# Sums of the up and down weights formed in DRAM by copies and adding transfers, in a fast-multiplication decoder layer on one core

## The chip, the cores and the metric

The kernel runs on one core of one Trainium2 chip. The metric is device time in microseconds (us); the kernel before took 1193.68 us, the median of three runs (1193.61 to 1193.87).

## The reference

One decoder layer over a sequence of 1024 positions and a model width of 1024, in float32. What matters here is its second half; the first half (attention over a window of 128, a spatial gating unit, two sigmoid gates, output projection) is computed as before.

```
merged = sigmoid(g_a) * (y_att @ w_oa) + sigmoid(g_b) * (y_sgu @ w_ob)
x = x + merged @ w_out
h = rmsnorm(x)
z = h @ w_up                              # 1024 x 5632
zc = causal depthwise convolution of z over 3 positions, plus a bias
gate, val = split(zc)                     # 2816 each
x = x + (silu(gate) * val) @ w_down       # 2816 x 1024
```

## The kernel before, in words

Every float32 operand is split into a high and a low part, and a product is three matmuls: high x high, high x low, low x high. The gate projections, the up projection and the down projection multiply two-by-two block matrices with seven block products instead of eight (a Strassen scheme of Winograd's form). So sums of weight blocks (S1 to S4) and sums of activation blocks (T1 to T4) stand beside the blocks themselves (A11 to A22, B11 to B22), and the products are put together by additions (`u2`, `x7`, `g0`, `g1`, `v0`, `v1`).

From v_phase on all engines run in the order in which the program is written; nothing is reordered. TensorE does the matmuls, VectorE (DVE) the sums of products, the convolution and some splits, ScalarE (ACT) the high parts and activations, GpSimd (POOL) the low parts and some weight sums. All transfers are issued by SyncE (SP) on one queue, and SP waits in order for whatever a transfer needs. The stages, one after the other:

- **Attention and SGU**, to about 221 us.
- **Gates** (`v_end`, `gate_pair`): eight pairs of gate tiles of 84 matmuls each. Per pair `load_p` and `load_q` bring the weights (`lp`, `lq`). POOL makes S3 and S1 from them (`sums_q`), then the low parts `pl` and `s3l`, then S2 and S4 (`sums_r`), then `ql` and the low part of S2 and S4 (`gax`). The gates' results go out to DRAM as `dth`.
- **Branches** (`branch`, `run_jobs`): sixteen tiles of 24 matmuls. For tile n SP loads a gate tile two ahead (`th`, 512 KB, 3 buffers) and a weight block four ahead (`wj`, 256 KB, tag `raw`, 3 buffers). ACT and POOL split the block two ahead (`wjh`, `wjl` at line 108, 2 buffers). DVE multiplies and adds.
- **Out** (`out_tile`, `last_tile`): eight tiles of 48 matmuls with weights of 512 KB; their results are normalized and split, with the sums T1 to T4.
- **Up** (`first_pair`, `fast_pair`): 22 pairs of column blocks of 84 matmuls each, in the order `U_ORDER`. `Left` holds one pair's weights: `p` (A11, A12), `q` (S1 and A22), `s3`, and `r` (S2, S4; made by POOL at line 620 through `sub`). Here S1 and S3 are read from DRAM (`load_q`, `load_s3`). `keep_act` writes the activations and their sums to DRAM.
- **Down** (`mlp`): seven block products M1 to M7, each over eleven blocks of 128 rows taken two at a time (a "group"). `loads` brings a group's weights and activations, `prep` splits them.

**Where the sums come from.** For the up stage, `sums_load` loads 256 KB and 512 KB of a pair's weights into a tile `ls` (2 buffers), `sums_step` makes two sums on DVE (line 620) and stores them as `sum<i>` in DRAM, 512 KB. `sums_step` runs twice in each of the gate pairs 2 to 7 and in ten of the sixteen branches. For the down stage `sum_loads` loads A21 and A22 of a group while M1 and M2 run, `sums2` makes S2 from them, and `prep` makes S3, S4 and S1, all on DVE. A11 and S2 stay in SBUF.

Of the kernel before, what the change touches and what calls it, by code (L numbers as in the profile page):

```python
# [10 lines left out]
F = mybir.dt.float32  # L11
# [30 lines left out]
def body(ctx, tc, nc, a):  # L42
# [217 lines left out]
    st = {}  # L260

# [360 lines left out]

    def x_gain(r, ks):
        for k in ks:
            x = xr_raw[r][:, k, :]
            nc.scalar.activation(x, x, AF.Copy, scale=cp[:, 186 + 4 * r + k:187 + 4 * r + k])

    def x_sums(ks, first):
        for k in ks:
            x0 = xr_raw[0][:, k, :]  # L630
            if first:
                sub(nc.vector, x0[:, L], x0[:, H], x0[:, L])
            else:
                x1 = xr_raw[1][:, k, :]
                sub(nc.vector, x0[:, H], x1[:, H], x0[:, H])
                sub(nc.vector, x1[:, H], x1[:, H], x0[:, L])
                sub(nc.vector, x1[:, L], x1[:, L], x1[:, H])
# [181 lines left out]
    def v_end():  # L819
# [53 lines left out]
        sums_load()  # L873
# [11 lines left out]
        nc.vector.tensor_tensor(x7, x7, e, op=ALU.add)  # L885
        nc.vector.tensor_tensor(q.g1, x5, q.g1, op=ALU.add)
        nc.vector.tensor_tensor(q.v1, x7, q.v1, op=ALU.add)
        nc.vector.tensor_tensor(q.v0, q.u2, q.v0, op=ALU.add)
# [39 lines left out]
    class Left:  # L928
# [8 lines left out]
        def load_q(self):  # L937
            if self.i is None:
                self.q = wload(self.sq, "lq")
                return  # L940
            self.q = raw("lq")
            nc.sync.dma_start(self.q[:, 0:4], pools["sum"][self.i][:, 1])
            nc.sync.dma_start(self.q[:, 4:8], self.sq[:, 4:8])

        def load_s3(self):
            self.s3 = pools["wx"].tile([128, 4, 128], F, tag="s3", name=nm("s3"))
            nc.sync.dma_start(self.s3, pools["sum"][self.i][:, 0])
# [9 lines left out]
        def sum_s3(self):  # L957
            self.s3 = s3_pool.tile([128, 4, 128], F, tag="s3", name=nm("s3"))
            sub(nc.gpsimd, self.s3, self.p[:, 0:4], self.q[:, 0:4])

        def sum_f3(self):

            sub(nc.gpsimd, self.p[:, 0:4], self.q[:, 4:8], self.r[:, 0:4])
# [15 lines left out]
        def sum_s2(self):  # L979
            self.r = raw("lr")  # L980
            sub(nc.gpsimd, self.r[:, 0:4], self.q[:, 0:4], self.p[:, 0:4])

        def sum_s4(self):
            sub(nc.gpsimd, self.r[:, 4:8], self.p[:, 4:8], self.r[:, 0:4])
# [26 lines left out]
    class Blocks:  # L1011
# [23 lines left out]
        def sums(self, x1, x7, m4):  # L1035

            nc.vector.tensor_tensor(self.v1, x1, self.v1, op=ALU.add)
            nc.scalar.copy(self.u2, self.v1)
            nc.vector.tensor_tensor(self.v0, self.u2, m4, op=ALU.add)
            nc.vector.tensor_tensor(self.v1, x7, self.v1, op=ALU.add)  # L1040
            self.scale(self.zv)
# [7 lines left out]

    sums = {"load": 0, "make": 0}  # L1050

    def sums_load():

        i = sums["load"]
        if i < NPAIR:
            x = pools["ls"].tile([128, 3, 4, 128], F, tag="ls", name=nm("ls"), bufs=2)
            nc.sync.dma_start(x[:, 0], a["wup"][2 * i][:, 0:4])
            nc.sync.dma_start(x[:, 1:3], a["wup"][2 * i + 1].rearrange("p (b k) m -> p b k m", b=2))
            sums[i] = x
            sums["load"] += 1  # L1060

    def sums_step():

        i = sums["make"]
        if i < NPAIR:
            sums_load()
            x = sums.pop(i)
            sub(nc.vector, x[:, 0], x[:, 0], x[:, 1])
            sub(nc.vector, x[:, 1], x[:, 1], x[:, 2], ALU.add)
            t = pools["dr"].tile([128, 2, 4, 128], F, tag=f"sum{i}", name=f"sum{i}")  # L1070
            nc.sync.dma_start(t, x[:, 0:2])
            pools.setdefault("sum", {})[i] = t
            sums["make"] += 1

# [27 lines left out]
    def gate_pair(c, prev):  # L1102
# [16 lines left out]
        if c > 1:  # L1119
            sums_step()  # L1120
# [75 lines left out]
    def branch(n):  # L1196
        br, c = B_ORDER[n]

        def main(w):
# [14 lines left out]
            if n % 2 == 0 or n in (5, 9):  # L1214
                sums_step()
# [38 lines left out]
    HK = NPAIR // 2  # L1254
# [11 lines left out]
    def out_tile(i):  # L1266
        d = D_ORDER[i]

        def main(w):
# [20 lines left out]
            if d < 4:  # L1290
                eng = nc.gpsimd if i < 6 else nc.vector
                right_split("B11", k, h[:, L], eng)
                sub(nc.vector, h[:, L], h[:, H], h[:, L])
                right_split("T1", k, h[:, L], eng)
            else:
                g = hs_[k]
                sub(nc.vector, g[:, H], h[:, H], g[:, H])
# [3 lines left out]
                t2 = sub(nc.vector, pools["raw2"][:, k, :], h[:, H], g[:, L])  # L1301
                sub(nc.vector, pools["raw4"][:, k, :], h[:, L], t2)
# [7 lines left out]
    def last_tile(w, ac):  # L1310
# [28 lines left out]
        sub(nc.vector, g[:, H], h[:, H], g[:, H])  # L1339
        right_split("B22", k, h[:, H], nc.vector)  # L1340
        right_split("T3", k, g[:, H], nc.vector)
        t2 = sub(nc.vector, pools["raw2"][:, k, :], h[:, H], g[:, L])
        sub(nc.vector, pools["raw4"][:, k, :], h[:, L], t2)
# [63 lines left out]
    def keep_act(i, tv):  # L1407
# [9 lines left out]
        if row == 0:  # L1417
            put("B11", tv[:, L])
            t1 = sub(nc.vector, tt(), tv[:, H], tv[:, L])
            put("T1", t1)  # L1420
            pools["prev"] = (tv, t1)
        else:
            g, t1 = pools["prev"]
            put("B21", tv[:, L])
            put("B22", tv[:, H])
            put("T3", sub(nc.vector, g[:, H], tv[:, H], g[:, H]))
# [4 lines left out]
    U_ORDER = [i for j in range(HK) for i in (j, j + HK)]  # L1431
    lefts = [Left(a["wup"][2 * i], a["wup"][2 * i + 1], i) for i in U_ORDER]

    def first_left():

        w = lefts[0]
        w.load_p()
        w.load_s3()
        w.load_q()
        yield  # L1440
        w.split_p()

    def first_pair():
# [32 lines left out]
        nc.vector.tensor_tensor(x7, x7, u2, op=ALU.add)  # L1476
# [11 lines left out]
        nc.vector.tensor_tensor(q.v1, u2, x7, op=ALU.add)  # L1488
        nc.vector.tensor_tensor(q.v0, u2, q.v0, op=ALU.add)
# [10 lines left out]
    def fast_pair(n, prev, q, hooks, rms=None):  # L1500
# [43 lines left out]
        nc.vector.tensor_tensor(x7, x7, q.g1, op=ALU.add)  # L1544
# [8 lines left out]
        if nx:  # L1553
            nx.split_q()
            nx.split_r(n + 1)
        else:
# [8 lines left out]
    SUM_AT = (2, 4, 5, 7, 8, 10)  # L1565
# [5 lines left out]
    def mlp():  # L1571
        groups = [(s, k0, k1) for s in STEPS for k0, k1 in GR]
        blk, ring = {}, {}
        zz = []

        def block(n, k0, k1):

            if k0 < 8:
                if n not in blk:
                    blk[n] = Y(n, F, [128, 8, 512])  # L1580
                return blk[n][:, k0:k1, :]
            if not zz:
                zz.append(pools["ex"].tile([128, 8, 512], F, tag="T3", name="zz"))
            b = 3 * ("A11", "S2").index(n) - 8
            return zz[0][:, b + k0:b + k1, :]

        def slot(n, dt, cnt):

            if n not in ring:
                y = pools["yd"].tile([128, 8, 512], F, name="rs") if n == "rs" else Y(n, dt, [128, 8, 512])  # L1590
                ring[n] = [y, 0]
# [3 lines left out]

        def a_in(n, t, k0, k1):
            r, c = int(n[1]) - 1, int(n[2]) - 1
            for k in range(k0, k1):
                nc.sync.dma_start(t[:, k - k0, :], a["wdown"][k + HK * c][:, 512 * r:512 * r + 512])

        raw_ = {}

        def loads(g):
# [15 lines left out]
        pre = {}  # L1619

        def sum_loads(k0, k1):
            pre[k0] = (block("S2", k0, k1), slot("rs", F, k1 - k0))
            a_in("A21", pre[k0][0], k0, k1)
            a_in("A22", pre[k0][1], k0, k1)

        def sums2(k0, k1):

            c, x = pre.pop(k0)
            sub(nc.vector, c, c, x, ALU.add)
            sub(nc.vector, c, c, block("A11", k0, k1))  # L1630

        def prep(g):
# [56 lines left out]
        def plus(n, d, p, last=False):  # L1689

            t = rs[n][:, d, :]
            nc.vector.scalar_tensor_tensor(t, p, 0.5, t, op0=ALU.mult, op1=ALU.add)
# [3 lines left out]
        def done(s):  # L1696
            for d in range(4):
# [4 lines left out]
                if s == "M6":  # L1702
                    plus("C21", d, X[d])
# [4 lines left out]
                if s == "M5":  # L1708
                    plus("C22", d, X[d], True)
# [33 lines left out]
        for g in range(len(groups)):  # L1743
# [5 lines left out]
            if g in SUM_AT:  # L1749
                sum_loads(*GR[SUM_AT.index(g)])  # L1750
# [16 lines left out]
            if g - 2 in SUM_AT:  # L1767
                sums2(*GR[SUM_AT.index(g - 2)])
# [12 lines left out]
def layout(x, mix_norm, w_in, q_norm, k_norm, sinks, sgu_norm, w_s, b_s,  # L1781
# [18 lines left out]
    wup = tiles(w_up, 8)[up_order]  # L1800

    def pcol(v):
# [10 lines left out]
    ali = -slopes[None, :, None] * dist[:, None, :]  # L1813
    return {
# [9 lines left out]
        "wup": wup,  # L1824
        "wdown": c(w_down.reshape(NPAIR, 128, 1024)),
# [20 lines left out]
```

## Time and profile before

| | before |
|---|---|
| time, median of 3 runs | 1193.68 us (1193.61 to 1193.87) |
| the profiled execution: its time / its span | 1193.8 us / 1192.1 us |
| TensorE (PE) busy | 1180.0 us, 99% of the span |
| VectorE (DVE) busy | 877.8 us, 74% |
| ScalarE (ACT) busy | 541.8 us, 45% |
| GpSimd (POOL) busy | 567.4 us, 48% |
| DMA, one queue | 190.26 MB, 45.9% of 16 engines' span |

The span runs from the first to the last instruction; the time also holds what lies around it. An engine's busy time is the sum of its instructions' spans. PEld is TensorE's loading of weights, which runs beside its matmuls. "DMA share" is the mean busy share of the core's 16 DMA engines. In rows of instructions the first column is the start in us, the second the duration; an arrow in brackets names what ended the idle time before.

### The profile page before, as it was taken

What the parts mean: (1) busy time and instruction counts of PE and PEld (TensorE: products, weight loads), DVE (VectorE), ACT (ScalarE), POOL (GpSimd) and SP (SyncE); (2) the same over time, 40 slices, a digit from 0 to 9 for tenths busy, and PEclk for the clock granted to TensorE, in tenths of its full rate; (3) what the DMA queues carried; (4) which work ended last, traced back from release to release, by engine and by line L of the source; (5) the groups of instructions that cost most, each with busy time, mean ns of one, the idle gap of its engine ahead of it and who ended that gap; (6) DMA issues with size and microseconds to landing.
All of it is one profiled execution on the core that took longest, in us unless ns stands there. A gap on an engine that the chain in (4) does not pass through costs nothing.

```text
span 1192.1 us, 15888 instructions
## 1 busy us (share of the span) xinstructions
PE 1180.0 (99%) x5890; PEld 1000.9 (84%) x5890; DVE 877.8 (74%) x1028; ACT 541.8 (45%) x832; POOL 567.4 (48%) x364
## 2 busy tenths in 40 slices
PE   8999999999999999999999999999999999999998
PEld 8989989988888888888888888888888888888887
DVE  7798975745638565668897788878788798865674
ACT  8555567644335222234544444444444445434331
POOL 2367685487768222343756575656657551000000
PEclk9999999999999999999999999999999999999999
DMA  7110133037786997342143342423333258966471
GB/s 272 35 54 19 54 136 130 5 130 260 245 315 212 347 327 278 125 165 100 54 142 108 104 143 98 148 91 124 108 131 124 89 209 290 373 230 194 151 233 67
DMA packets 79134, 191.27 MB, mean 160 GB/s; under 512 B 8913, under 2 KB 9169, under 8 KB 79057
## 3 DMA queue, kind: packets, MB, share of 16 engines
q1 hardware_dynamic: 79056, 190.26, 45.9%
q8 instruction: 46, 0.75, 0.3%
q14 instruction: 32, 0.25, 0.1%
HBM read 139.63 MB, written 50.59 MB: 160 GB/s over the span
## 4 chain that ended last, share of the span: by engine, by line
PE 89%; DVE 4%; POOL 1%; issue 1%; ACT 0%; POOLq 0%; DVEq 0%; ACTq 0%
PE pz L1028 48%; PE pd L1672 10%; PE pdy L1672 8%; PE px L93 2%; PE px L92 2%; PE po L93 2%; PE po L92 2%; PE po L91 2%; PE px L91 2%; PE pvs L91 1%; PE pvs L92 1%; PE pvs L93 1%; DVE ya L529 1%; PE pq L91 1%; PE pq L93 1%; PE pq L92 1%
## 5 line engine op out<-in xcount | busy, mean ns | idle before, releaser
L1028 PE MATMUL pz<-T,qh 128*128 128x512 f32 x472 | 145.6, 390 | 0.0
L988 POOL TENSOR_TENSOR pl<-lp,ph 128x1024 fp32r<-128x1024 f32 x30 | 72.5, 2418 | 83.5 <-ACT ph L87 83.3
L1028 PE MATMUL pz<-B,ph 128*128 128x512 f32 x352 | 109.1, 391 | 0.0
L1028 PEld LDWEIGHTS pz<-T,qh 128*128 128x128 f32 x472 | 88.5, 188 | 18.6 <-ACT u L879 0.3
L1028 PE MATMUL pz<-T,ql 128*128 128x512 f32 x236 | 91.8, 389 | 0.0
L108 POOL TENSOR_TENSOR wjl<-wj,wjh 128x512 fp32r<-128x512 f32 (+1 forms) x24 | 40.6, 1692 | 95.8 <-ACT wjh L87 95.8
L988 POOL TENSOR_TENSOR ql<-lq,qh 128x1024 fp32r<-128x1024 f32 x30 | 76.9, 2565 | 9.1 <-ACT qh L87 9.1
L1028 PEld LDWEIGHTS pz<-B,ph 128*128 128x128 f32 x352 | 65.3, 188 | 15.0 <-ACT x L1519 1.8
L1044 DVE TENSOR_TENSOR pz<-pz,rstd_b 128x1024 f32<-128x1024 f32 x60 | 73.9, 1232 | 4.2 <-ACT rstd_b L141 2.1
L988 POOL TENSOR_TENSOR s3l<-s,s3h 128x512 fp32r<-128x512 f32 x29 | 39.8, 1373 | 69.7 <-ACT s3h L87 69.7
L1028 PE MATMUL pz<-T,s3h 128*128 128x512 f32 x232 | 71.4, 389 | 0.0
L1028 PE MATMUL pz<-B,pl 128*128 128x512 f32 x176 | 68.6, 390 | 0.0
L1672 PE MATMUL pd<-bl,ah 128*128 128x512 f32 x176 | 68.5, 389 | 0.0
L1672 PE MATMUL pd<-bh,ah 128*128 128x512 f32 x176 | 68.5, 389 | 0.0
L1672 PE MATMUL pd<-bh,al 128*128 128x512 f32 x176 | 68.5, 389 | 0.0
L1028 PE MATMUL pz<-T,AX 128*128 128x512 f32 x264 | 63.4, 389 | 0.0
L1028 PE MATMUL pz<-B,AX 128*128 128x512 f32 x264 | 63.4, 389 | 0.0
L1028 PEld LDWEIGHTS pz<-T,AX 128*128 128x128 f32 x264 | 49.6, 188 | 10.3
L1028 PEld LDWEIGHTS pz<-B,AX 128*128 128x128 f32 x264 | 49.6, 188 | 10.3
L1378 DVE SCALAR_TENSOR_TENSOR tg<-pz,cp,tg 128x1023 f32<-128x1023 f32 (+1 forms) x44 | 56.2, 1278 | 0.8
L1378 DVE SCALAR_TENSOR_TENSOR tv<-pz,cp,tv 128x1023 f32<-128x1023 f32 (+1 forms) x44 | 56.2, 1277 | 0.8
L988 POOL TENSOR_TENSOR AX<-lr,AX 128x1024 fp32r<-128x1024 f32 x22 | 53.7, 2440 | 5.1 <-ACT AX L87 5.1
(342 smaller groups left out, 3511.8 us busy)
## 6 DMA issues: line engine op xcount, KB each, us to landing
ls<-wup SPq DMA_DIRECT2D x22, 512.0 KB, 5.3
sum<-ls SPq DMA_DIRECT2D x22, 512.0 KB, 5.3
lp<-wup SPq DMA_DIRECT2D x22, 512.0 KB, 3.6
ra<-wdown SPq DMA_DIRECT2D x44, 256.0 KB, 4.6
b<-T SPq DMA_DIRECT2D x44, 256.0 KB, 3.8
B<-tv SPq DMA_DIRECT2D x33, 256.0 KB, 2.0
T<-tt SPq DMA_DIRECT2D x33, 256.0 KB, 2.0
b<-B SPq DMA_DIRECT2D x33, 256.0 KB, 3.1
```

The lines of the kernel that those rows point to most:

```text
L91: nc.tensor.matmul(out, wh, mh, start=first, stop=False, **kw)
L92: nc.tensor.matmul(out, wh, ml, start=False, stop=False, **kw)
L93: nc.tensor.matmul(out, wl, mh, start=False, stop=last, **kw)
L108: nc.gpsimd.tensor_tensor(l[:, :nk, :], r[:, :nk, :], h[:, :nk, :].bitcast(F), op=ALU.subtract)
L529: nc.vector.tensor_tensor(ya[r, 2 * half:2 * half + 2, b * 128:(b + 1) * 128], p[r, g], o[r], op=ALU.add)
L988: nc.gpsimd.tensor_tensor(l, r, h.bitcast(F), op=ALU.subtract)
L1028: nc.tensor.matmul(o, p[:, k, :], y[:, q, k, :], start=not more and k == 0 and j == 0, stop=k == 3 and j == 2, skip_group_check=True)
L1044: nc.vector.tensor_tensor(z, z, rstd_b, op=ALU.mult)
L1378: nc.vector.scalar_tensor_tensor(t[:, j:], p[:, 0:1024 - j], cw[:, ci, 2 - j:3 - j], t[:, j:], op0=ALU.mult, op1=ALU.add)
L1672: nc.tensor.matmul(o[d], p[:, k - k0, m], q[:, k - k0, :], start=new and k == 0 and j == 0, stop=k == HK - 1 and j == 2, skip_group_check= ...
```

## The change

Three edits belong together.

1. **The sums for the up stage.** DVE no longer makes them. For pair i, ACT issues a copy of two blocks of `w_up` (512 KB) within DRAM into `sum<i>`, and POOL issues a transfer that adds two other blocks to it there. The copies run up to three pairs ahead of the adds; an add waits for its copy. `sums_step` now runs once in each of gate pairs 1 to 7 and once in each branch. The tile `ls` and its loads and stores are gone. The blocks of `w_up` lie in memory in a new order, so that one transfer covers two of them; `load_p` reads two pieces of 2 KB per partition where it read one of 4 KB.
2. **The sums for the down stage.** In the up stage `fast_pair` calls `down_step` once per pair: 12 copies on ACT (1 MB, the last ones 512 KB) and 18 adds on POOL (1 MB or 512 KB, the last ones half). All of S1 to S4 then lie in DRAM. `loads` reads each group's weights, block or sum, in one transfer into the ring `ra`; `sum_loads`, `sums2` and the subtractions in `prep` are gone.
3. **Signs.** The transfers can add but not subtract, so some sums of weights change sign. The sums of activations and the additions of products change sign with them: a `tensor_tensor` with its operands swapped or with add for subtract, and in 19 places `neg_sum`, a `scalar_tensor_tensor`, for a subtraction.

The matmuls, their number and their order are the same.

```diff
+    def rows4k(t):
+        return t.rearrange("(p b) m -> p (b m)", b=2)
+    todo = {"copy": 0, "add": 0}
+    def sums_step():
+        j = todo["add"]
+        while todo["copy"] < min(j + 3, NPAIR):
+            sum_copy(U_ORDER[todo["copy"]])
+            todo["copy"] += 1
+        if j < NPAIR:
+            sum_add(U_ORDER[j])
+            todo["add"] += 1
+    def sum_copy(i):
+        sums[i] = dr.tile([256, 512], F, tag=f"sum{i}", name=f"sum{i}")
+        nc.scalar.dma_start(rows4k(sums[i]), rows4k(a["wup"][i, 0:2].rearrange("b p m -> (b p) m")))
+    def sum_add(i):
+        nc.gpsimd.dma_start(rows4k(sums[i]), rows4k(a["wup"][i, 1:3].rearrange("b p m -> (b p) m")), accum_op=ALU.add, max_dma_last_dim=4096)
...
+    def neg_sum(out, x, y):
+        nc.vector.scalar_tensor_tensor(out, x, -1.0, y, op0=ALU.mult, op1=ALU.subtract)
+        return out
...
@@ Left
-            nc.sync.dma_start(self.q[:, 0:4], pools["sum"][self.i][:, 1])
-            nc.sync.dma_start(self.q[:, 4:8], self.sq[:, 4:8])
+            nc.sync.dma_start(self.q[:, 0:4], sums[self.i][128:256])
+            nc.sync.dma_start(self.q[:, 4:8], self.sq)
...
@@ gate_pair
         gate_out(("b", c - 1), prev.zg)
-        if c > 1:
-            sums_step()
+        sums_step()
         q.prod(q.v0, "S3", "T3")
...
-        nc.vector.tensor_tensor(x7, x7, q.g1, op=ALU.add)
+        sub(nc.vector, x7, x7, q.g1)
         if nx:
             nx.sums_r()
-        if c > 1:
-            sums_step()
...
@@ branch
-            if n % 2 == 0 or n in (5, 9):
-                sums_step()
+            sums_step()
...
@@ keep_act
-            t2 = sub(nc.vector, tt(), tv[:, H], t1)
+            t2 = neg_sum(tt(), t1, tv[:, H])
             put("T2", t2)
-            put("T4", sub(nc.vector, tt(), tv[:, L], t2))
+            put("T4", sub(nc.vector, tt(), tv[:, L], t2, ALU.add))
...
+    D_ADDS = [(i, j) for j in range(6) for i in range(3)]
+    D_COPIES = [(i, j) for j in range(6) for i in (1, 0)]
+    def down_copy(i, j):
+        t = d_sum[i, j] = dr.tile([256, 1024 if j < 5 else 512], F, tag=f"sd{i}{j}", name=f"sd{i}{j}")
+        nc.scalar.dma_start(t, wd(j, i, i + 2))
+    def down_add(i, j):
+        x, y = d_sum[1, j], d_sum[0, j]
+        out, src = ((x, wd(j, 2, 4)), (y[128:256], x[128:256]), (y[0:128], y[128:256]))[i]
+        nc.gpsimd.dma_start(out, src, accum_op=ALU.add, max_dma_last_dim=4096)
+    def down_step(n):
+        if n < len(D_COPIES):
+            down_copy(*D_COPIES[n])
+        if 0 <= n - 2 < len(D_ADDS):
+            down_add(*D_ADDS[n - 2])
...
@@ fast_pair
             nx.split_q()
             nx.split_r(n + 1)
+            down_step(n - 1)
...
@@ mlp
-            x = None
-            if s == "M1":
-                x = block("A11", k0, k1)
-                a_in("A11", x, k0, k1)
-            elif s not in ("M5", "M6"):
-                x = slot("ra", F, n)
-                a_in({"M2": "A12", "M7": "A22", "M4": "A22", "M3": "A12"}[s], x, k0, k1)
+            x = slot("ra", F, n)
+            a_in(LHS[s], x, k0, k1)
...
-            if s == "M6":
-                x = block("S2", k0, k1)
-            elif s in ("M7", "M3"):
-                sub(nc.vector, x, x, block("S2", k0, k1))
-            elif s == "M5":
-                x = block("A11", k0, k1)
-                sub(nc.vector, x, x, block("S2", k0, k1), ALU.add)
...
-            if g in SUM_AT:
-                sum_loads(*GR[SUM_AT.index(g)])
...
-            if g - 2 in SUM_AT:
-                sums2(*GR[SUM_AT.index(g - 2)])
```

More of the change, by code (lines that the diff above doesn't have):

```diff
@@ L260, in body @@
     st = {}
+    sums = {}
+    HK = NPAIR // 2
+    U_ORDER = [i for j in range(HK) for i in (j, j + HK)]
+    def rows4k(t):
[14 more added lines that the diff above has]
+        nc.gpsimd.dma_start(rows4k(sums[i]), rows4k(a["wup"][i, 1:3].rearrange("b p m -> (b p) m")), accum_op=ALU.add, max_dma_last_dim=4096)
     def q_proj(n):
@@ L1038, in sums @@
             nc.scalar.copy(self.u2, self.v1)
[L1039 to L1040 removed]
+            sub(nc.vector, self.v0, m4, self.u2)
+            sub(nc.vector, self.v1, x7, self.v1)
             self.scale(self.zv)
@@ L1048, in last_sum @@
             self.scale(self.zg)
[L1050 to L1073, printed above, removed]
     jobs.clear()
@@ L1300, in main @@
                 right_split("T3", k, g[:, H], nc.vector)
-                t2 = sub(nc.vector, pools["raw2"][:, k, :], h[:, H], g[:, L])
-                sub(nc.vector, pools["raw4"][:, k, :], h[:, L], t2)
+                t2 = neg_sum(pools["raw2"][:, k, :], g[:, L], h[:, H])
+                sub(nc.vector, pools["raw4"][:, k, :], h[:, L], t2, ALU.add)
             if i == 0:
@@ L1338, in last_tile @@
         g = hs_[k]
-        sub(nc.vector, g[:, H], h[:, H], g[:, H])
+        sub(nc.vector, g[:, H], g[:, H], h[:, H])
         right_split("B22", k, h[:, H], nc.vector)
         right_split("T3", k, g[:, H], nc.vector)
-        t2 = sub(nc.vector, pools["raw2"][:, k, :], h[:, H], g[:, L])
-        sub(nc.vector, pools["raw4"][:, k, :], h[:, L], t2)
+        t2 = neg_sum(pools["raw2"][:, k, :], g[:, L], h[:, H])
+        sub(nc.vector, pools["raw4"][:, k, :], h[:, L], t2, ALU.add)
     late = {}
@@ L1425, in keep_act @@
             put("B22", tv[:, H])
-            put("T3", sub(nc.vector, g[:, H], tv[:, H], g[:, H]))
-            t2 = sub(nc.vector, tt(), tv[:, H], t1)
+            put("T3", sub(nc.vector, g[:, H], g[:, H], tv[:, H]))
+            t2 = neg_sum(tt(), t1, tv[:, H])
             put("T2", t2)
-            put("T4", sub(nc.vector, tt(), tv[:, L], t2))
-    U_ORDER = [i for j in range(HK) for i in (j, j + HK)]
-    lefts = [Left(a["wup"][2 * i], a["wup"][2 * i + 1], i) for i in U_ORDER]
+            put("T4", sub(nc.vector, tt(), tv[:, L], t2, ALU.add))
+    lefts = [Left(a["wup"][i, 0::3].rearrange("b p m -> p b m"), a["wup"][i, 2], i) for i in U_ORDER]
     def first_left():
@@ L1475, in first_pair @@
         nx.split_s3()
-        nc.vector.tensor_tensor(x7, x7, u2, op=ALU.add)
+        sub(nc.vector, x7, x7, u2)
         q.prod(q.g1, "S4", "B22", more=True)
@@ L1487, in first_pair @@
         q.u2 = u2
-        nc.vector.tensor_tensor(q.v1, u2, x7, op=ALU.add)
-        nc.vector.tensor_tensor(q.v0, u2, q.v0, op=ALU.add)
+        sub(nc.vector, q.v1, x7, u2)
+        sub(nc.vector, q.v0, q.v0, u2)
         def rms():
@@ L1543, in fast_pair @@
             nx.split_p()
-        nc.vector.tensor_tensor(x7, x7, q.g1, op=ALU.add)
+        sub(nc.vector, x7, x7, q.g1)
         if rms:
@@ L1572, in mlp @@
         groups = [(s, k0, k1) for s in STEPS for k0, k1 in GR]
[L1573 to L1585, printed above, removed]
+        ring = {}
         def slot(n, dt, cnt):
             if n not in ring:
-                y = pools["yd"].tile([128, 8, 512], F, name="rs") if n == "rs" else Y(n, dt, [128, 8, 512])
-                ring[n] = [y, 0]
+                ring[n] = [Y(n, dt, [128, 8, 512]), 0]
             y, i = ring[n]
@@ L1594, in slot @@
             return y[:, 2 * (i % 4):2 * (i % 4) + cnt, :]
+        SRC = {"A12": 0, "A11": 1, "A22": 3, "S3": (1, 0), "S1": (1, 1), "S4": (0, 0), "S2": (0, 1)}
         def a_in(n, t, k0, k1):
-            r, c = int(n[1]) - 1, int(n[2]) - 1
-            for k in range(k0, k1):
-                nc.sync.dma_start(t[:, k - k0, :], a["wdown"][k + HK * c][:, 512 * r:512 * r + 512])
+            j = k0 // 2
+            if n[0] == "A":
+                src = wd(j, SRC[n], SRC[n] + 1)
+            else:
+                i, b = SRC[n]
+                src = d_sum[i, j][128 * b:128 * b + 128]
+            nc.sync.dma_start(t.rearrange("p k m -> p (k m)"), src)
         raw_ = {}
@@ L1687, in put, with plus @@
             nc.sync.dma_start(a["out"][4 * r + d, :, 512 * c:512 * c + 512], t)
-        def plus(n, d, p, last=False):
+        def plus(n, d, p, last=False, by=0.5):
             t = rs[n][:, d, :]
-            nc.vector.scalar_tensor_tensor(t, p, 0.5, t, op0=ALU.mult, op1=ALU.add)
+            nc.vector.scalar_tensor_tensor(t, p, by, t, op0=ALU.mult, op1=ALU.add)
             if last:
@@ L1702, in done @@
                 if s == "M6":
-                    plus("C21", d, X[d])
+                    plus("C21", d, X[d], by=-0.5)
                 if s == "M7":
@@ L1708, in done @@
                 if s == "M5":
-                    plus("C22", d, X[d], True)
+                    plus("C22", d, X[d], True, -0.5)
                 if s == "M3":
```

55 lines of the change are left out of this document (25 added, 30 removed).

## The prediction

> **What bounds the kernel now.** I read the page's first part, then busy time by stage, then the chain of waits, then the DMA view of the stage that the change loads most.
>
> ```profile
> span 1192.1 us, 15888 instructions
> ...
> PE 1180.0 (99%) x5890; PEld 1000.9 (84%) x5890; DVE 877.8 (74%) x1028; ACT 541.8 (45%) x832; POOL 567.4 (48%) x364
> ```
>
> The profiled execution took 1193.8 us, 1.7 more than its span and 0.1 above the median of the three runs (1193.68); the sum below is made against 1193.8. The two stretches of the next view cut the span where the TensorE stops waiting.
>
> ```profile
> core 0: us, PE busy (x) PEld busy (x) DVE busy (x) ACT busy (x) POOL busy (x), PEclk, DMA share, GB/s
> 0.00:200.00 200.00, 192.05 (x1407) 179.69 (x1408) 156.33 (x319) 127.42 (x333) 116.29 (x124) 1.00 0.29 104
> 200.00:1186.00 986.00, 986.00 (x4478) 819.99 (x4478) 718.80 (x707) 414.41 (x499) 451.09 (x240) 1.00 0.50 172
> ```
>
> From 200 us to 1186 us TensorE is busy for 986.00 of 986 us. All of its idle time lies in the first 200 us (8.0 us, start and attention) and after the last matmul. A busy engine could still be a slowed one, so I took its pace from the chain of waits:
>
> ```profile
> 244.64 136.26 PE pz L1028 x600
> ...
> 580.39 397.86 PE pz L1028 x1752
> 978.24 29.92 PE pd L1672 x132
> ...
> 1185.91 2.73 DVE res L1692 x4
> ```
>
> Per matmul that is 136.26/600 = 0.2271 us in the gates, 397.86/1752 = 0.2271 in the up stage and 29.92/132 = 0.2267 in the down stage. If 0.2267 is the floor, 2352 matmuls hide 0.0004 x 2352 = 0.9 us. **So the change can win about 1 us**: no matmul is removed, and whatever is taken from VectorE (DVE) or from SP's queue comes out of engines that TensorE does not wait for. What it can lose is open.
>
> **The change part by part: what goes away.** The 44 halves of the up sums:
>
> ```profile
> L620 DVE TENSOR_TENSOR ls<-ls 128x512 f32<-128x512 f32 x44 | 44.5, 1010 | 9.4 <-DMA ls<-wup 8.6
> L620 DVE TENSOR_TENSOR tt<-tv,tt 128x512 f32<-128x512 f32 x22 | 35.8, 1625 | 0.4
> L1692 DVE SCALAR_TENSOR_TENSOR res<-pd,res 128x512 f32<-128x512 f32 x12 | 8.2, 691 | 13.3 <-PE pd L1672 13.3
> ```
>
> 44.5 us leave DVE in gates and branches, and 30 subtractions leave it in the down stage. TensorE ran full beside all of them: 0 us. The signs cost nothing either: an add for a subtract is the same instruction; the 19 `neg_sum` replace subtractions (mean 1.625 us, row two) by an operation whose nearest row of that size is 0.691. Even twice 1.625 would put 1.6 us into a pair of 19 us, of which DVE is idle for 3.4 (up stage, 296.55 of 360 in the rows below). The down stage reads as many bytes as before (77 blocks of 256 KB), two to a transfer.
>
> ```profile
> 247.00:380.50 133.50, 133.50 (x590) 110.54 (x589) 75.15 (x78) 58.82 (x72) 102.68 (x59) 1.00 0.68 233
> 380.50:468.00 87.50, 87.50 (x387) 72.47 (x386) 54.51 (x55) 20.06 (x26) 28.34 (x18) 1.00 0.85 309
> ...
> 600.00:960.00 360.00, 360.00 (x1587) 297.01 (x1586) 296.55 (x284) 163.33 (x190) 221.35 (x113) 1.00 0.35 117
> 978.00:1186.00 208.00, 208.00 (x919) 171.88 (x918) 143.77 (x140) 82.16 (x92) 7.55 (x4) 1.00 0.65 221
> ```
>
> These rows are gates, branches, up and down stage; the columns from the third on are busy PE, PEld, DVE, ACT, POOL, then clock, DMA share and GB/s. Full speed of the transfers is 309/0.85 = 363 GB/s, so a plain 512 KB (0.524 MB) costs **1.44 us** of all DMA engines, 256 KB 0.72.
>
> **What is added: where the transfers land.** `sums_step` runs once in each of gate pairs 1 to 7 and once in each branch: gates get 9 copies and 7 adds, branches 13 copies (in branches 0 to 12) and 15 adds; the up stage gets 12 copies (11.5 MB) and 18 adds (11.5 MB). No row shows a copy from DRAM to DRAM or an add. A copy is bounded by 1.44 (one pass) and 2.88 (its read and its write each paid); an add, which reads two sources and writes one, by 1.44 and 4.32. A copy is nearest to a load, 1.44. An add is nearest to two loads, 2.88. Both ends stay for the range.
>
> Gates: the old sums there were 15.2 MB of 31.1, so 15.9 MB (44 us) stay; even 9 x 2.88 + 7 x 4.32 = 56 us more make 100 of 133.5. Up stage, over 381 us: 117 GB/s is 44.6 MB; counting copies twice and adds three times (57 MB) gives 102 of 138. Both fit, hidden beside TensorE. **The branches are the tight place:**
>
> ```profile
> DMA packets 8994, 27.00 MB, mean 309 GB/s; under 512 B 1008, under 2 KB 1008, under 8 KB 8988
> ...
> th<-dth SPq DMA_DIRECT2D x16, 512.0 KB, 6.2
> sum<-ls SPq DMA_DIRECT2D x10, 512.0 KB, 5.2
> ls<-wup SPq DMA_DIRECT2D x9, 512.0 KB, 5.3
> ls<-wup SPq DMA_DIRECT2D x9, 256.0 KB, 4.4
> wj<-woa SPq DMA_DIRECT2D x7, 256.0 KB, 6.3
> ```
>
> The old sums are 10 x 0.524 + 9 x 0.786 = 12.3 of these 27 MB. In their place come 28 transfers of 0.524, 14.7 MB if each counted once. Per branch of 5.44 us the DMA engines get `th` and `wj`, 1.44 + 0.72 = 2.16, plus 1.44 + 2.88: **6.48 us of work**, 1.04 too much, in 13 branches 13.5 us.
>
> What this costs TensorE is less, since loads run ahead:
>
> ```profile
> 429.72 0.63 ACT L87 ACTIVATE wjh<-wj 128x512 fp32r<-128x512 f32 x1 [1.05 <-PE po L92]
> 435.16 0.63 ACT L87 ACTIVATE wjh<-wj 128x512 fp32r<-128x512 f32 x1 [4.81 <-PE po L92]
> ...
> 430.43 1.30 POOL L108 TENSOR_TENSOR wjl<-wj,wjh 128x512 fp32r<-128x512 f32 x1 [4.10 <-ACT wjh L87]
> ```
>
> A branch starts near 429.7, the next 5.44 later; the split of the block for the branch after is ready at 431.73, 3.4 us before that branch. The block four ahead is loaded from the moment its slot is free (2.0 into a branch) and wanted three branches later, 14.3 us on; landing takes 6.3, which leaves 8.0, and with the 3.4 it may be 11.4 us late, once. Queued behind one copy and one add (4.32) it has 7.1 left. 13.5 - 7.1 = **6.4 us** of TensorE waiting.
>
> By the Trainium skill (DMA: Bandwidth & Descriptors, Issuing engines are not separate DMA queues) transfers started by ACT, SP or GpSimd run on the same 16 engines and interleave, so moving the sums off SP's queue buys no bandwidth. No trace here shows another queue than SP's. If the rule failed, and the added queues had engines of their own, the 6.4 us would be 0.
>
> **What is added: waits and issue.** In pair 1 three copies are issued at once on ACT and the first add waits on POOL for the first of them. Behind it on POOL stand the sums and splits for pair 2:
>
> ```profile
> 254.18 1.02 ACT L1083 ACTIVATE th<-pz 128x1024 f32<-128x1024 f32 x1
> ...
> 254.79 2.42 POOL L988 TENSOR_TENSOR gax<-lr,gax 128x1024 fp32r<-128x1024 f32 x1
> 259.10 1.29 POOL L620 TENSOR_TENSOR s<-lp,lq 128x512 f32<-128x512 f32 x1 [1.88 <-DMA lq<-wga]
> 260.46 1.29 POOL L620 TENSOR_TENSOR lq<-lq 128x512 f32<-128x512 f32 x1
> 261.71 2.40 POOL L988 TENSOR_TENSOR pl<-lp,ph 128x1024 fp32r<-128x1024 f32 x1
> ...
> 266.68 0.19 PEld L1028 LDWEIGHTS pz<-x,pl 128*128 128x128 f32 x1
> ```
>
> The copy is issued at 255.2. How long 512 KB take to land, and an issue on a free and on a crowded queue, stand in the view of DMA issues and in SP's timeline:
>
> ```profile
> x<-ac SPq DMA_DIRECT2D x8, 512.0 KB, 2.7
> ```
>
> ```profile
> 270.37 0.33 SPq L97 DMA_DIRECT2D lq<-wga  x1
> ...
> 272.75 2.04 SPq L1058 DMA_DIRECT2D ls<-wup  x1
> ```
>
> Between 2.7 and the 6.2 of `th` above it lands at 257.9 to 261.4, middle 259.7. What an add holds POOL for is not shown: below it costs an issue of SP (0.33), above twice the longer POOL split here (4.8); I take the short split, 1.3. POOL resumes at 261.0 rather than 259.1, 1.9 late, and `pl` was done 2.6 before PEld took it (266.68 - 264.11): 0. At the upper ends POOL is 7.1 late, 4.5 us lost. I charge **0.6**, since `lq` itself now shares the engines with three copies. Later adds find their copy 38 us old in the gates, about 11 in the branches. In a branch POOL has 1.3 of 5.44 us to do, so an add up to 4.1 us is hidden; in the up stage 221.35 of 360 leaves 7.3 us of each pair of 19.05, in the gates 102.68 of 133.5 leaves 4.4. ACT's copies are 0.33 to 2.04 us of issue beside 20.06 of 87.5 us busy: hidden.
>
> The Trainium skill (DMA: Bandwidth & Descriptors, Specifications) gives about 1 us to the first byte of a transfer issued from GpSimd; that as price would also be hidden.
>
> **Sum:** 1193.8 + 0 (DVE, signs, down stage) + 0.6 (first add) + 6.4 (branches) = **1200.8 us**.
>
> **Rivals.**
> 1. *It fits, no slower.* If the two transfers of a branch cost under 4.0 us together, 13 x (2.16 + 4.0 - 5.44) = 9.4 less the remaining cushion of 7.4 is 2 us or less. For it: at 1.44 each the branch needs 5.04 of 5.44, and 0.85 share already ran without a stall. Against: an add has two sources. It gives 1194.4.
> 2. *Every pass through DRAM is paid.* Copy 2.88, add 4.32: 13 x (9.36 - 5.44) = 51 less 4.2, so 1241; half way up (copy 2.16, add 3.6), 13 x 2.48 = 32 less 5.6, 1221. For it: both ends of these transfers are DRAM, of none in the trace. The Trainium skill (DMA: Bandwidth & Descriptors, Latency and other measured facts) has 214 GB/s for copies from HBM to HBM, 2.45 us for 512 KB as an estimate; with an add of 2.88 that would be 1215.
> 3. *POOL is held.* An add that keeps POOL over 4.1 us (slow issue, or waiting on landings) delays `wjl` in 15 branches: at 6 us 15 x (1.3 + 6 - 5.44) = 28 less 3.4 gives 1219. Against: POOL is idle for two thirds of the stage.
> 4. *Faster.* Only through the first 200 us, which the change barely touches, or the 0.9 us of pace.
>
> **How the numbers follow.** Forecast, 1196.2 to 1208: 0.38. Rival 1: 0.34. Rival 2, from 1208 up: 0.18. Rival 3: 0.06. Rival 4: 0.04. A measurement here tells 0.2% (2.4 us) from no change. Slower 0.38 + 0.18 + 0.06 = 0.62, same 0.34, faster 0.04. The range 1193.0 to 1218.0 leaves out rival 4 and about half of rivals 2 and 3, 0.16.
>
> **What would show it.** Right: TensorE gaps between 380 and 500 us that end on ACT `wjh` or POOL `wjl`, behind them a late `wj`; DMA share near 1 there; gates, up and down stage still without a gap. Rival 1: no gap, share below 1. Rival 2: gaps of 2 us and more in each branch. Rival 3: a gap released by POOL while `wj` had landed long before. Wrong altogether: gaps in the up stage, or a different pace per matmul.

## The result, and where the profile after puts the time

The changed kernel takes **1231.6 us**, the median of four runs (1230.4 to 1232.9), against 1193.6 for the kernel before on the same chip: 1.0319 times as long (95% interval 1.0301 to 1.0337), and above the range that was forecast. The profiled execution took 1232.9 us, 39.1 more than that of before. First the head of the page of the changed kernel:

```profile
span 1231.2 us, 15752 instructions
...
PE 1194.5 (97%) x5890; PEld 1005.5 (82%) x5890; DVE 804.4 (65%) x954; ACT 542.0 (44%) x832; POOL 591.8 (48%) x404
```

DVE lost 73 us of work, and the matmuls are as many as before; still TensorE is busy 14.5 us longer, with 24.6 us more of idle span. So part of the loss is idle time and part is a slower pace. Busy time by stage shows where (branches, out, up and down stage; columns as before):

```profile
385.00:480.00 95.00, 92.96 (x404) 75.03 (x403) 40.51 (x32) 19.31 (x25) 36.03 (x32) 1.00 1.03 320
480.00:583.00 103.00, 103.00 (x470) 85.73 (x469) 77.06 (x68) 38.29 (x51) 45.29 (x24) 1.00 0.33 116
583.00:1016.00 433.00, 410.54 (x1755) 333.03 (x1754) 329.00 (x314) 181.12 (x211) 255.13 (x141) 0.98 0.56 165
1020.00:1225.00 205.00, 204.41 (x902) 168.69 (x901) 107.78 (x107) 79.33 (x90) 5.08 (x2) 1.00 0.64 221
```

The same stretch of the up stage in the kernel before:

```profile
580.40:978.20 397.80, 397.80 (x1753) 328.11 (x1753) 329.58 (x315) 181.99 (x212) 241.31 (x123) 1.00 0.36 121
```

**Nearly all of it lies in the up stage.** Its matmuls took 397.8 us and now take 433.0, 35.2 more: 433.0 - 410.5 = 22.5 us of gaps, and 410.5 - 397.8 = 12.7 us of slower matmuls at a granted clock of 0.98. The branches lost 2.0 us in gaps and 404 x 0.2271 = 91.7 of 93.0 in pace, 3.3 in all; the down stage 0.6. That is the 39.1. The DMA share of the up stage is only 0.56, so the stage didn't run out of DMA engines. The waits of the up stage say who was late:

```profile
ACT s3h L87 <- DMA s<-sum: 70.7, 15, 8.9
PE pz L1056 <- ACT x L1554: 21.9, 8, 5.6
```

(waiter, releaser: us in all, times, longest.) TensorE waited eight times for ScalarE's copy `x7` (line 1554), and ScalarE had waited for the load `s` (S3 of the next pair), one of the sums that the change forms by transfers. In the kernel before that wait was 4.8 us in all. The timeline of one pair, cut to the instructions that matter, shows the order of events:

```profile
637.56 0.50 ACTq L1449 DMA_DIRECT2D sd<-wdown  x1
639.91 0.32 SPq L970 DMA_DIRECT2D lq<-sum  x1
640.27 2.98 SPq L971 DMA_DIRECT2D lq<-wup  x1
642.18 0.95 POOL L1455 DMA_DIRECT2D sd<-wdown  x1
643.30 0.43 SPq L975 DMA_DIRECT2D s<-sum  x1
652.58 0.63 ACT L87 ACTIVATE s3h<-s 128x512 fp32r<-128x512 f32 x1 [7.66 <-DMA s<-sum]
653.11 0.57 ACT L1554 COPY x<-pz 128x512 f32<-128x512 f32 x1
...
653.73 0.77 PE L1056 MATMUL pz<-T,qh 128*128 128x512 f32 x2 [4.28 <-ACT x L1554]
```

`down_step` issues a 1 MB copy on ACT and a 1 MB add on POOL at the end of a pair, within 6 us of SP's loads `lq` and `s` for the next pair. `s` reaches ACT at 652.5. ACT's queue is in order, so the copy that TensorE needs stands behind the split of `s`. How the pace fell: the 5 us behind this gap, and the 5 us behind the next one, of 1.36 us:

```profile
653.73:658.73 5.00, 5.00 (x15) 3.97 (x16) 4.05 (x5) 2.39 (x3) 3.91 (x3) 0.66 0.15 57
676.03:681.03 5.00, 5.00 (x22) 4.14 (x23) 3.94 (x4) 2.92 (x3) 3.90 (x3) 1.00 0.14 54
```

Behind the gap of 4.28 us TensorE is busy for the whole 5 us and does 15 matmuls instead of 22, at a granted clock of 0.66: 1.6 us more lost. Behind the other long gaps (5.59, 5.04 and 3.27 us) it does 13, 12 and 15, at 0.56, 0.50 and 0.66; behind the four short ones (0.49 to 1.36 us) it does 22 at 1.00. The four long gaps so cost 33 matmuls, 7.5 of the 12.7 us, some 1.9 us each on top of their idle time. The rest is spread over the stage and was not traced. The Trainium skill (TensorE: Matmul & The Clock Gate, HAM oscillation) warns of TensorE idle for over about 3.4 us, after which the clock starts low. Three of the four long gaps agree; the one of 3.27 us lowered the clock as well, so here that length is no sharp limit (experiment 5 has a gap of 1.79 us that did).

### The profile page after: what moved, and what is told of

Its sections match the earlier page's. It is cut to its first block, busy times and chain, and to the rows that moved or that the text cites. A ratio compares the mean times of both kernels' runs of the same rounds, so it can differ in the third digit from the quotient of the medians.

```text
span 1231.2 us, 15752 instructions
## 1 busy us (share of the span) xinstructions
PE 1194.5 (97%) x5890; PEld 1005.5 (82%) x5890; DVE 804.4 (65%) x954; ACT 542.0 (44%) x832; POOL 591.8 (48%) x404
## 3 DMA queue, kind: packets, MB, share of 16 engines
q0 software_dynamic: 6272, 23.07, 10.2%
q10 hardware_dynamic: 1088, 23.07, 5.3%
## 5 line engine op out<-in xcount | busy, mean ns | idle before, releaser
L1056 PE MATMUL pz<-T,qh 128*128 128x512 f32 x472 | 152.7, 406 | 22.0 <-ACT x L1554 21.9
L1056 PEld LDWEIGHTS pz<-T,qh 128*128 128x128 f32 x472 | 91.2, 196 | 45.6 <-ACT x L1554 26.5
L1056 PE MATMUL pz<-T,ql 128*128 128x512 f32 x236 | 94.8, 402 | 0.0
L1637 DVE TENSOR_TENSOR al<-ra,ah 128x1024 fp32r<-128x1024 f32 (+1 forms) x42 | 49.2, 1171 | 60.0 <-ACT ah L87 60.0
L87 ACT ACTIVATE ah<-ra 128x1024 fp32r<-128x1024 f32 (+1 forms) x42 | 41.5, 988 | 97.0 <-PE pd L1662 43.7
L1398 DVE SCALAR_TENSOR_TENSOR pz<-pz,tg 128x1024 f32<-128x1024 f32 x22 | 27.1, 1233 | 57.6 <-ACT pz L1395 57.6
L87 ACT ACTIVATE s3h<-s 128x512 fp32r<-128x512 f32 x29 | 18.2, 629 | 95.7 <-DMA s<-sum 70.7
```

The lines of the kernel that those rows point to most:

```text
L87: return nc.scalar.activation(dst, src, AF.Copy, scale=scale)
L1056: nc.tensor.matmul(o, p[:, k, :], y[:, q, k, :], start=not more and k == 0 and j == 0, stop=k == 3 and j == 2, skip_group_check=True)
L1398: nc.vector.scalar_tensor_tensor(self.zv, self.zg, 1.0, self.tg, op0=ALU.add, op1=ALU.mult)
L1637: eng.tensor_tensor(l, t, h.bitcast(F), op=ALU.subtract)
```

## The experiments

All compared with the kernel before on the same chip. **Theory A:** bytes fit, but copy and add at the end of a pair make `s` land late, and ACT's order hands that on to TensorE. **Theory B:** there are too many bytes. **Theory C:** the changed signs, or POOL's issue of the adds, slow the stage. Where an expectation gives a letter a narrower meaning, it says so.

**1. `mid_pair`: the same transfers, half a pair later.**

```diff
             nx.split_r(n + 1)
-            down_step(n - 1)
...
         nc.scalar.copy(x7, q.v0)
+        if nx:
+            down_step(n - 1)
```

> Changed kernel, with down_step moved within fast_pair from the end of a pair (just ahead of SP's loads of lq and s) to behind the x7 copy, when these loads have landed. The same copies, adds, bytes and signs. Theory A (collision with the loads of s): the up stage returns to about 423 us, the branches keep their 3.5 us: 1195 to 1199 us. Theory B (too many transfers): 1215 to 1232, since no transfer is gone. Theory C (signs, POOL's issue): 1228 to 1232.

Measured: 1198.4 us, 1.0046 (1.0031 to 1.0061). Its windows (branches, up stage) and the same pair on the timeline:

```profile
385.00:475.00 90.00, 87.95 (x379) 71.66 (x378) 38.86 (x31) 18.62 (x25) 35.55 (x32) 0.98 1.03 318
580.00:980.00 400.00, 399.95 (x1769) 329.67 (x1768) 330.62 (x316) 182.03 (x212) 257.26 (x143) 1.00 0.62 179
```

```profile
640.66 0.43 SPq L975 DMA_DIRECT2D s<-sum  x1
645.05 0.63 ACT L87 ACTIVATE s3h<-s 128x512 fp32r<-128x512 f32 x1 [0.23 <-DMA s<-sum]
645.59 0.57 ACT L1554 COPY x<-pz 128x512 f32<-128x512 f32 x1
...
649.26 0.62 PE L1056 MATMUL pz<-T,qh 128*128 128x512 f32 x2
```

The up stage has no gap, at a *higher* DMA share (0.62 against 0.56): not the bytes but their moment. Signs and adds are as they were, so theory C is out as well. The two timelines give the gap as a sum. In the changed kernel `s` was issued at 643.30 instead of 640.66, 2.6 us later, because SP's issue of `lq` took 2.98 us instead of 0.43; and it took 9.2 us (to 652.5) instead of 4.3 to arrive, 4.9 more. Together 7.5 us. `x7` is ready at 646.16 here and wanted at 649.26, a cover of 3.1. So 4.4 us should show, and 4.28 did.

**2. `x7_first`: let `x7` go ahead of the split.**

```diff
-        if nx:
-            nx.split_s3()
         nc.scalar.copy(x7, q.v0)
+        if nx:
+            nx.split_s3()
```

> Changed kernel, with one pair of lines in fast_pair swapped: ACT copies x7 out of PSUM before it splits S3, so that ACT's wait for the block s no longer stands ahead of x7. Theory A (the copy and the add of down_step delay the load of s, ACT waits for s ahead of the x7 copy, TensorE waits for x7, and its granted clock falls after each gap): the gaps released by the x7 copy are gone; what remains is the chain s, s3l, pl on POOL, which in the worst pair ended 1.4 us after the next pair could have started, so about 1198 to 1206 us. Theory B (the up stage has more transfers than the DMA engines can carry): TensorE's gaps stay under another name, 1222 to 1232. Theory C (the changed signs or POOL's issue of the adds slow the stage): 1228 to 1232.

Measured: 1224.2 us, 1.0264 (1.0248 to 1.0279). A miss: the number that A gave is far off. The waits of its up stage:

```profile
ACT s3h L87 <- DMA s<-sum: 58.9, 14, 8.6
PE pz L1056 <- DVE x L645: 13.6, 7, 3.9
PE pz L1056 <- ACT x L1540: 5.6, 5, 1.5
```

`s` is as late as before, and TensorE no longer waits for `x7` but for what stands behind the split on ACT: the activations, then DVE's work on them, then DVE's `x7 - g1`. One instruction moved ahead of a blocked queue only changes which of the others is late first.

**3. `s3_late`: the split of `s` still later.**

```diff
-        if nx:
+        if nx and rms:
             nx.split_s3()
...
         if nx and not rms:
             nx.split_p()
+            nx.split_s3()
```

> Changed kernel with down_step where it was, but the split of S3 moved in fast_pair behind the split of p, so that on ACT x7, tanh and the high part of p, and on POOL the low part of p, no longer stand behind the wait for s. The swap of x7 alone gained only 7 us; its trace shows the wait moved on to tanh, which stands behind the same wait, and through DVE (gated, then x7 - g1) to TensorE. Theory A in its wider form (the late s holds up all that stands behind it on ACT, POOL and DVE; the collision itself is harmless): the up stage's gaps vanish although s still lands as late: 1196 to 1201 us. If instead late lq or lp hold the stage, or the engines are overfull (theory B), it stays above 1212.

Measured: 1225.2 us, 1.0261 (1.0246 to 1.0276), a miss again, for another reason. Waits of its up stage, and its window:

```profile
PE pz L1056 <- ACT x L1540: 21.4, 19, 1.8
ACT s3h L87 <- DMA s<-sum: 4.7, 3, 1.8
```

```profile
580.00:980.00 400.00, 380.06 (x1662) 309.02 (x1661) 308.14 (x295) 168.89 (x201) 242.46 (x134) 1.00 0.55 166
```

The wait for `s` is gone, but now all 19 pairs stall by 1.1 us each: the later split delays POOL's chain of low parts and sums, and through it ACT and DVE. The order itself is a constraint here, so this run says nothing of the collision. It does bear on the clock: gaps of up to 1.8 us, 19 times, and the clock stayed at 1.00 behind them.

**4. `s3_first`: issue `s` ahead of `lq`.** This is the clean test: the orders of ACT, POOL, DVE and TensorE and all transfers stay.

```diff
         if nx:
-            nx.load_q()
             nx.load_s3()
+            nx.load_q()
```

> Only the order of two loads on SP is changed: in a pair of the up stage `s` is issued ahead of `lq` and so does not wait for the buffer of `lq`. In the profile of the changed kernel that wait is some 2.3 us and `lq` itself 0.7 to 3.3 us of issue (`lp` issued at 637.55, `lq` at 639.91, `s` at 643.30), so `s` goes 3 to 5 us earlier and ahead of the add of that pair (POOL, 642.18). Every copy, every add and every instruction of TensorE, ScalarE, VectorE and POOL keeps its place and its bytes. Theory A (copy and add at the end of a pair make `s` land too late, ScalarE stands waiting for it ahead of the copy x that TensorE needs): `s` was about 4 us too late in the pairs with a gap, so the waits of ScalarE for `s` fall from 70.7 us to under 20, the up stage runs with at most 3 us of gaps at clock 1.00, and the time is 1196 to 1201 (branches +3.5, perhaps some pairs where `lq`, now the later one, delays the split for ScalarE). Theory B (the collision delays more than `s`: `lq`, or the transfers of B and T, stop TensorE as well): 1205 to 1228, and the gap moves to another wait. The rate of the transfers would be no answer to either, since none is taken away.

Measured: 1206.1 us, 1.0103 (1.0087 to 1.0118). That is 25 us better than the changed kernel by the order of two issues, but 5 above what A gave. Waits in its up stage, and rows of its timeline:

```profile
ACT s3h L87 <- DMA s<-sum: 22.5, 6, 6.7
...
PE pz L1056 <- ACT x L1554: 4.6, 2, 3.4
```

```profile
697.60 0.50 ACTq L1449 DMA_DIRECT2D sd<-wdown  x1
698.56 0.38 SPq L97 DMA_DIRECT2D lp<-wup  x1
699.06 3.75 SPq L975 DMA_DIRECT2D s<-sum  x1
702.68 0.90 POOL L1455 DMA_DIRECT2D sd<-wdown  x1
```

What is left ends on the same wait; B's other loads don't appear. In the pairs that still stall SP takes 3.4 to 4.2 us to issue `s` itself, behind a copy that ACT has just issued. So `s` late is the cause, and issuing it first cures it only where SP isn't held.

**5. One part at a time.** `no_sums` leaves out all copies and adds, `no_down` those for the down stage (both read weight blocks of the same size in place of the sums), `copies_only` the adds for the down stage; `adds_only` issues the down copies in the out stage instead.

```diff
 # no_sums
     def sums_step():
+        return
 # no_sums, no_down
-            down_step(n - 1)
 # copies_only
-        if 0 <= n - 2 < len(D_ADDS):
-            down_add(*D_ADDS[n - 2])
 # adds_only
-        if n < len(D_COPIES):
-            down_copy(*D_COPIES[n])
...
+            if i < 6:
+                down_copy(*D_COPIES[2 * i])
+                down_copy(*D_COPIES[2 * i + 1])
             p = PS("px")
```

> Changed kernel with no copy and no add at all: both kinds of sums are left out, and blocks of the weights of the same size are read in their place. What remains of the change are the signs, the other layout and the work taken from DVE and from SP. Theories A and B: 1192.5 to 1194.5, no gain from the work that left DVE, since TensorE did not wait for it. Theory C: above 1215.

> Changed kernel without down_step: no copy and no add in the up stage, and the down stage reads blocks of w_down of the same size where it read the sums, so the sums of w_down are left out. Theories A and B: up stage at about 423 us, total 1195 to 1199. Theory C (signs): 1225 to 1232. The difference to the time of the one before is then what the branches, the first stages and the signs cost together.

> Changed kernel with the copies of down_step at their place and its adds left out (so the down stage reads copies in place of sums). By the share of their queue, the copies take 1.48 us of the DMA engines for 512 KB, so 3.0 us for 1 MB. In the kernel before, s could land about 5 us later without a gap. Theory A: s lands at most 3 us later, no gap in the up stage, 1196 to 1200 us. Theory B (the sum of bytes): half of the bytes, so about half of the loss, 1210 to 1220.

> Changed kernel with the adds of down_step at their place, and its copies issued in the out stage instead (two in each of six tiles). The adds take 2.85 us of the DMA engines for 512 KB, 5.7 for 1 MB. Theory A: the ten of 512 KB stay under the 5 us that s has, the five of 1 MB are at the edge, so a few small gaps: 1197 to 1206 us; neither part alone gives the 35 us, which come from both together. Theory B: 1212 to 1222.

| kernel | us | ratio (95% interval) |
|---|---|---|
| `no_sums` | 1193.8 | 1.0005 (0.9995 to 1.0014) |
| `no_down` | 1198.2 | 1.0044 (1.0028 to 1.0061) |
| `copies_only` | 1202.7 | 1.0072 (1.0057 to 1.0087) |
| `adds_only` | 1198.4 | 1.0040 (1.0025 to 1.0055) |

`no_sums` lacks all the added transfers and has all the rest (DVE's lighter load, the signs): no change, so these cost and win nothing. `no_down` prices the up sums, about 5 us. By the ratios the down copies alone add 0.0028 to it, 3.3 us (the time is a little over the upper end expected), and the adds alone nothing; **both together, in the changed kernel, add 0.0275, 33 us**. Why so much more than the sum is seen in the wait of ACT for `s`. `copies_only`:

```profile
ACT s3h L87 <- DMA s<-sum: 33.6, 16, 5.0
PE pz L1056 <- ACT x L1552: 2.2, 2, 1.8
```

`adds_only`, where no wait of TensorE is listed:

```profile
ACT s3h L87 <- DMA s<-sum: 5.6, 9, 1.1
```

With copies alone `s` is up to 5.0 us late, and a cover of about 3 hides nearly all of it; with both it is up to 8.9 us late, beyond the cover, and the fall of the clock comes on top. (The expectations gave `s` 5 us; the cover is nearer to 3.) The changed kernel shows the same within its own up stage: the copies end at 843.1 us and the adds go on to 1001.6, and all eight gaps lie before 836. One gap of `copies_only`, of only 1.79 us, also lowered the clock, where 19 gaps of up to 1.80 us in `s3_late` did not; the 5 us behind it:

```profile
747.41:752.41 5.00, 5.00 (x15) 4.00 (x16) 3.92 (x4) 2.40 (x3) 3.90 (x3) 0.66 0.14 52
```

So the length of a gap alone does not decide it; what else does stays open.

**6. `mid_old_pace`: `mid_pair` with the up sums at their old pace** (two steps in each of gate pairs 2 to 7, ten in the branches), to get the branches back.

```diff
-        sums_step()
+        if c > 1:
+            sums_step()
...
         if nx:
             nx.sums_r()
+        if c > 1:
+            sums_step()
...
-            sums_step()
+            if n % 2 == 0 or n in (5, 9):
+                sums_step()
```

> The kernel mid_pair with the up sums' steps at the old places: two in each of the gate pairs 2 to 7, ten in the branches. If the branches' 3 to 4 us come from DMA engines with more work than a branch is long (2.16 + 1.48 + 2.85 = 6.5 us for 5.44), then with 10 adds and 8 copies in 16 branches the work is 2.16 + 2.5 = 4.7 a branch and the gaps vanish: 1193 to 1195 us. If they come from an add standing on POOL ahead of wjl, or from the copies on ACT, each of the ten adds still costs: 1195 to 1198.

Measured: 1201.6 us, 1.0065 (1.0048 to 1.0081). The branches ran without a gap, as expected, but the gates now lost more than was won; waits there:

```profile
POOL s L645 <- DMA lq<-wga: 29.2, 6, 7.2
PE pz L1056 <- POOL pl L1016: 5.7, 3, 3.0
```

By these waits the second step of a pair meets SP's load `lq`, which POOL needs first: the same kind of collision in another stage.

**7. `mid_spread`: every sum where nothing near it is wanted soon.** `mid_pair`, and the up sums in the gates as in the changed kernel, in every second branch, and seven in the out stage.

```diff
-            sums_step()
+            if n % 2 == 0:
+                sums_step()
...
+            if i < 7:
+                sums_step()
             p = PS("px")
```

> As `mid_pair` (copy and add of the down sums issued in the middle of a pair), and the sums of the up weights at another pace: one step in each gate pair as in the changed kernel, one in every second branch (8, not 15), and the other 7 in the first seven tiles of the output stage, where the profile of before shows a DMA share of 0.37. All the work of the change is done. Theory A (time is lost only where transfers meet a load that is wanted soon): the branches get 1.44 + 2.88 us in every second one, about 4.3 of 10.9 us beside 2 x 2.16 of loads, which fits, and the output stage gets 7 x 4.3 = 30 us beside 0.37 x 87 = 32 of 87 us, which fits: 1193 to 1196, no gap over 0.5 us from 380 to 980 us. Theory B (each sum formed by transfers costs TensorE something wherever it stands): 1197 to 1202, as `mid_pair` at 1198.4.

Measured over eleven runs: **1193.8 us, 1.0005 (0.9996 to 1.0014)**: no difference from the kernel before. Gates, branches, out and up stage:

```profile
205.00:385.00 180.00, 179.49 (x884) 151.92 (x884) 82.08 (x102) 87.62 (x113) 128.13 (x80) 1.00 0.49 148
385.00:475.00 90.00, 90.00 (x399) 74.53 (x398) 39.09 (x32) 19.82 (x25) 30.92 (x26) 1.00 0.88 270
475.00:580.00 105.00, 105.00 (x481) 87.48 (x480) 77.11 (x68) 38.43 (x52) 50.49 (x30) 1.00 0.61 175
580.00:980.00 400.00, 399.97 (x1761) 329.26 (x1760) 331.55 (x317) 182.98 (x213) 256.38 (x142) 1.00 0.61 179
```

All copies and adds of the change, and 38 us of the loss gone: the loss was in the moments of issue alone.

**8. `s3_spread`: `s3_first` with that pace.**

> The order of `s3_first` (`s` ahead of `lq`, copies and adds of the down sums at the end of a pair) with the pace of the up sums of `mid_spread`. Theory A: what is left of the loss of `s3_first` in the branches goes, so 3 to 5 us less than `s3_first` and 1193 to 1198. Theory B: the output stage, with fourteen transfers more, shows gaps of its own, and the time is that of `s3_first` or more.

Measured: 1199.9 us, 1.0051 (1.0037 to 1.0065): 6 us less than `s3_first`, a little more than expected, and 2 above the range; the rest is the up stage's, 395.5 busy of 400 us.

No run beat the kernel before, and none could by much: `no_sums` has none of the work and takes the same time.

## Why the prediction was wrong, point by point

- **What bounds the kernel** (right). TensorE does; a lighter DVE won nothing (`no_sums`).
- **DVE's sums, the signs, `neg_sum`, the down stage: 0 us** (right to 0.6 us).
- **Prices of copy and add: 1.44 and 2.88 us of all DMA engines** (right). The page of the changed kernel has the adds (q0, the kind that POOL issues) and the copies (q10, ACT's) by queue: packets, MB, share of 16 engines' span.

```profile
q0 software_dynamic: 6272, 23.07, 10.2%
q10 hardware_dynamic: 1088, 23.07, 5.3%
```

23.07 MB are 44 units of 512 KB. 0.102 x 1231.2 / 44 = 2.85 us an add, 0.053 x 1231.2 / 44 = 1.48 a copy. By the 214 GB/s that the Trainium skill (DMA: Bandwidth & Descriptors, Latency and other measured facts) gives for copies between HBM tensors whose row pitch is padded, a copy was estimated at 2.45; for the copies here the measurement decides against it.
- **First add in pair 1: 0.6 us** (0). POOL waited for the copy and was on time all the same:

```profile
258.15 1.04 POOL L285 DMA_DIRECT2D sum<-wup  x1 [1.68 <-DMA sum<-wup]
258.96 1.57 POOL L645 TENSOR_TENSOR s<-lp,lq 128x512 f32<-128x512 f32 x1
```

POOL's next sum began at 258.96, not at 261.0. Its price for an add, taken as 1.3 us, was 0.8 to 1.0.
- **Branches: 6.4 us** (right in mechanism, too large). The waits of TensorE and the loads there, of the changed kernel:

```profile
PE po L93 <- POOL wjl L108: 1.2, 2, 0.6
PE po L91 <- ACT wjh L87: 0.7, 2, 0.5
```

```profile
th<-dth SPq DMA_DIRECT2D x16, 512.0 KB, 12.3
```

The waits end where I put them, at a DMA share of 1.03, and `th` landed in 12.3 us instead of 6.2. So SP's loads land later beside transfers from ACT and POOL. That agrees with the Trainium skill (DMA: Bandwidth & Descriptors, Issuing engines are not separate DMA queues), by which they all run on the same 16 engines and interleave. With fewer copies and adds per branch (`mid_old_pace`, `mid_spread`) the gaps are gone. The stage lost 3.3 us, not 6.4. The prices of copy and add held, so by subtraction the cushion was some 10 us and not 7.1; no run measured it by itself.
- **Up stage: "Both fit, hidden beside TensorE"** (the step that failed). By bytes they do fit, as `mid_pair` and `mid_spread` prove. But I compared a stage's sum of DMA time with the stage's length, and never asked when the transfers start. I did ask it for the branches, where each load got a due time and a cushion; for the up stage I didn't write down that `s` has only some 3 us. `down_step` puts a copy of 1 MB and an add of 0.5 or 1 MB, 3.0 + 2.9 to 5.7 us of all engines, right beside that load. My "gaps in the up stage" stood only in the list of what would prove me wrong, without a chance or a price. It cost 35 us: 22.5 of gaps, and 12.7 of pace, a term that I had nowhere.
- **The rivals.** None is what happened. Rival 2 had part of the time range (1221 to 1241) by another mechanism, twice the price in the branches, which the prices above refute; that the measured time falls into it is luck. Rival 3 needed POOL held for over 4.1 us an add.

## What to carry to other kernels

An average share of the DMA engines says whether transfers fit, not whether they are harmless: for each added transfer, list the loads issued within its landing time, their slack, and what stands behind their consumer on an in-order queue. Where a small load with a few us of slack is near, issue the large transfer right after that load has landed; here that moved 33 us with no byte changed. Price a long gap of TensorE above its idle time: here one of 4.28 us cost nearly 6, while those of up to 1.36 us cost little more than their length.

## What was not expected of the hardware

- **SP's issue is slow shortly after a copy on ACT's queue.** It took 0.3 to 0.4 us as a rule. In every pair of the changed kernel with a copy of 1 MB at its end an issue of SP took 2.5 to 3.2 us (`copies_only`: 2.5 to 3.0; `s3_first`: up to 4.2), mostly ending 5.2 to 5.9 us after the copy's issue. Behind the last two copies, of 512 KB, `lq` took 1.4 to 1.7 us in the changed kernel and in `copies_only`. In `adds_only`, with no copy in the up stage, `lq` and `s` took at most 0.53. So a transfer on another queue seems to delay SP itself, besides sharing the engines. But long issues occur with SP's queue alone too (one of 2.04 us in the gates of the kernel before, one of 1.95 for `s` in `no_sums`), so the link is argued from when they come, and why is open.
- **An add lands late.** Beside the other traffic 512 KB took 9.3 us (median) from issue to landing, a copy 6.5, while their shares of the engines are 2.85 and 1.48 us.
